# A row-mean kernel: the last tile's chunks summed by VectorE alone with a chained two-source instruction

## The chip, the cores and the metric

The kernel runs on 1 core of one Trainium2 chip. The metric is the device time of one execution in microseconds (us). The jobs ran on different chips (the record numbers them 13, 9, 2 and 4), so the verdicts rest on times of the same job.

Because the change works on the last 8 us or so, I also use a **tail**, read from the timeline of a trace. It runs from the start of the VectorE reduction of 128x4096 (I call that moment T0) to the issue of the last output store. That reduction starts when the last whole-tile load has landed, and the change does not touch it. The tail therefore leaves out all differences in the load stream before T0. A chunk's **landing** is the moment at which the trace records the load's last semaphore update; the `--critical` view ends a DMA piece there.

## The reference

```python
def setup_inputs():
    return {"x": np.random.randn(64, 256, 8192).astype(np.float32)}

def reference(x):
    return np.mean(x, axis=2)
```

These are 16384 rows of 8192 numbers, 537 MB read, and one mean per row written.

## The kernel before

Rows go on the 128 partitions. 63 loads bring two rows per partition each (128x16384). VectorE sums 62 of them with one reduction each and shares the 63rd with ScalarE. Then follow two tiles of 128 rows. The first comes in one load and is split between VectorE and ScalarE. The last comes in four chunks of falling size, so that little work is left when the last byte lands. The parts that the change touches:

```python
CH = [9 * L // 16, L // 4, L // 8, L // 16]      # 4608, 2048, 1024, 512 columns
...
s0 = CH[0] // 2 - L // 64                        # VectorE's share of chunk 0: 2176 columns
s1 = CH[1] // 2                                  # and of chunk 1: 1024
...
# VectorE
eng.wait_ge(one_sem, 16)
eng.tensor_reduce(res1[:, 0:1], buf1[:, : L // 2], X, ADD).then_inc(dve_sem, 1)   # 128x4096: T0
eng.wait_ge(ch_sems[0], 16)
eng.tensor_reduce(part[:, 0:1], buf2[:, :s0], X, ADD).then_inc(dve_sem, 1)
eng.wait_ge(ch_sems[1], 16)
eng.tensor_reduce(part[:, 1:2], buf2[:, offs[1] : offs[1] + s1], X, ADD).then_inc(dve_sem, 1)
eng.wait_ge(ch_sems[3], 16)
eng.tensor_reduce(part[:, 2:3], buf2[:, offs[3] : offs[3] + CH[3]], X, ADD).then_inc(dve_sem, 1)
eng.wait_ge(dve_sem, NP + 4)
eng.wait_ge(act_sem, 5)
eng.wait_ge(prep_sem, 1)
eng.tensor_reduce(fin[:, 0:1], part[:, 0:6], X, ADD).then_inc(fin_sem, 1)      # merge
eng.wait_ge(fin_sem, 1)
eng.transpose(fint[:], fin[:]).then_inc(fin_sem, 1)                            # column to rows
eng.wait_ge(fin_sem, 2)
eng.tensor_scalar(fint[:], fint[:], inv, None, mult).then_inc(fin_sem, 1)      # scale by 1/L
...
# ScalarE: the rest of chunks 0 and 1, and all of chunk 2, by accumulating copies
eng.wait_ge(ch_sems[0], 16)
acc(part[:, 3:4], buf2[:, s0 : CH[0]])
eng.wait_ge(ch_sems[1], 16)
acc(part[:, 4:5], buf2[:, offs[1] + s1 : offs[1] + CH[1]])
eng.wait_ge(ch_sems[2], 16)
acc(part[:, 5:6], buf2[:, offs[2] : offs[2] + CH[2]])
...
# SyncE: the last store
eng.wait_ge(fin_sem, 3)
eng.dma_start(out_q[4 * T2 : 4 * T2 + 4, :], fint[0:P:32, :])
```

Of the kernel before, what the change touches and what calls it, by code (L numbers as in the profile page):

```python
# [6 lines left out]
def bass_global_avg_pool_1d_kernel(  # L7
# [4 lines left out]
    P = 128  # L12
    B, C, L = x.shape
    rows = B * C
    inv = 1.0 / float(L)
    f32 = mybir.dt.float32
    ADD = mybir.AluOpType.add
    X = mybir.AxisListType.X
# [6 lines left out]
    assert rows % (R * P) == 0  # L25
    NP = rows // (R * P) - 1
    NBUF = 3
    CH = [9 * L // 16, L // 4, L // 8, L // 16]
    assert sum(CH) == L
    NCH = len(CH)  # L30

# [10 lines left out]
    with ExitStack() as ctx:  # L42
        E = ctx.enter_context
        bufs = [E(nc.sbuf_tensor(f"buf{i}", [P, R * L], f32)) for i in range(NBUF)]
        res = E(nc.sbuf_tensor("res", [P, NP, R], f32))
        res1 = E(nc.sbuf_tensor("res1", [P, 2], f32))
        part = E(nc.sbuf_tensor("part", [P, 8], f32))
        fin = E(nc.sbuf_tensor("fin", [P, 32], f32))
        fint = E(nc.sbuf_tensor("fint", [P, 32], f32))
        ident = E(nc.sbuf_tensor("ident", [P, P], f32))  # L50
        outsb = E(nc.sbuf_tensor("outsb", [NP, P, R], f32))
        out1sb = E(nc.sbuf_tensor("out1sb", [1, P], f32))
        ps = [E(nc.psum_tensor(f"ps{r}", [NP, P], f32)) for r in range(R)]
        psone = E(nc.psum_tensor("psone", [1, P], f32))

        in_sems = [E(nc.semaphore(f"in_sem{i}")) for i in range(NBUF)]
        one_sem = E(nc.semaphore("one_sem"))
        ch_sems = [E(nc.semaphore(f"ch_sem{i}")) for i in range(NCH)]
        dve_sem = E(nc.semaphore("dve_sem"))
        act_sem = E(nc.semaphore("act_sem"))  # L60
        prep_sem = E(nc.semaphore("prep_sem"))
        pe_sem = E(nc.semaphore("pe_sem"))
        cp_sem = E(nc.semaphore("cp_sem"))
        fin_sem = E(nc.semaphore("fin_sem"))
        out_sems = [E(nc.semaphore(f"out_sem{i}")) for i in range(3)]

        b1 = NP % NBUF
        b2 = (NP + 1) % NBUF
        buf1 = bufs[b1]
        buf2 = bufs[b2]  # L70
        offs = [sum(CH[:i]) for i in range(NCH)]
        s0 = CH[0] // 2 - L // 64
        s1 = CH[1] // 2

        def gpsimd_program(eng):
            eng.memset(fin[:], 0.0).then_inc(prep_sem, 1)  # L76
            eng.memset(ident[:], 0.0).then_inc(prep_sem, 1)  # L77
            eng.wait_ge(prep_sem, 2)
            eng.affine_select(  # L79
                out=ident[:],  # L80
                in_=ident[:],
                compare_op=mybir.AluOpType.not_equal,
                fill=1.0,
                base=0,
                pattern=[[-1, P]],
                channel_multiplier=1,
            ).then_inc(prep_sem, 1)

        first = len(nc.main_func.blocks[0].instructions)

        def sync_program(eng):
            for t in range(NP):
                if t >= NBUF:
                    eng.wait_ge(dve_sem, t - NBUF + 1)
                eng.dma_start(bufs[t % NBUF][:], x_pair[t]).then_inc(in_sems[t % NBUF], 16)  # L95
            eng.wait_ge(dve_sem, NP - NBUF + 1)
            eng.dma_start(buf1[:, :L], x_one[T1]).then_inc(one_sem, 16)
            eng.wait_ge(dve_sem, NP - NBUF + 2)
            for c in range(NCH):
                sl = slice(offs[c], offs[c] + CH[c])  # L100
                eng.dma_start(buf2[:, sl], x_one[T2][:, sl]).then_inc(ch_sems[c], 16)  # L101

            eng.wait_ge(cp_sem, 2)
            eng.dma_start(out_pair[0:NP, :], outsb[:].rearrange("t p r -> t (p r)")).then_inc(
                out_sems[0], 16
            )
            eng.wait_ge(cp_sem, 3)
            eng.dma_start(out_one[T1 : T1 + 1, :], out1sb[:]).then_inc(out_sems[1], 16)
            eng.wait_ge(fin_sem, 3)
            eng.dma_start(out_q[4 * T2 : 4 * T2 + 4, :], fint[0:P:32, :]).then_inc(  # L110
                out_sems[2], 16
            )
            for s in out_sems:
                eng.wait_ge(s, 16)

        def vector_program(eng):
            for t in range(NP - 1):
                eng.wait_ge(in_sems[t % NBUF], 16 * (t // NBUF + 1))
                eng.tensor_reduce(  # L119
                    res[:, t, :],  # L120
                    bufs[t % NBUF][:].rearrange("p (r l) -> p r l", r=R),
                    X,
                    ADD,
                ).then_inc(dve_sem, 1)
            t = NP - 1
            eng.wait_ge(in_sems[t % NBUF], 16 * (t // NBUF + 1))
            eng.tensor_reduce(res[:, t, 0:1], bufs[t % NBUF][:, :L], X, ADD).then_inc(dve_sem, 1)  # L127
            eng.wait_ge(one_sem, 16)
            eng.tensor_reduce(res1[:, 0:1], buf1[:, : L // 2], X, ADD).then_inc(dve_sem, 1)  # L129
            eng.wait_ge(ch_sems[0], 16)  # L130
            eng.tensor_reduce(part[:, 0:1], buf2[:, :s0], X, ADD).then_inc(dve_sem, 1)  # L131
            eng.wait_ge(ch_sems[1], 16)
            eng.tensor_reduce(  # L133
                part[:, 1:2], buf2[:, offs[1] : offs[1] + s1], X, ADD
            ).then_inc(dve_sem, 1)
            eng.wait_ge(ch_sems[3], 16)
            eng.tensor_reduce(  # L137
                part[:, 2:3], buf2[:, offs[3] : offs[3] + CH[3]], X, ADD
            ).then_inc(dve_sem, 1)
            eng.wait_ge(dve_sem, NP + 4)  # L140
            eng.wait_ge(act_sem, 5)
            eng.wait_ge(prep_sem, 1)
            eng.tensor_reduce(fin[:, 0:1], part[:, 0:6], X, ADD).then_inc(fin_sem, 1)  # L143
            eng.wait_ge(fin_sem, 1)
            eng.transpose(fint[:], fin[:]).then_inc(fin_sem, 1)  # L145
            eng.wait_ge(fin_sem, 2)
            eng.tensor_scalar(  # L147
                fint[:], fint[:], inv, None, mybir.AluOpType.mult
            ).then_inc(fin_sem, 1)

        def scalar_program(eng):
            def acc(dst, src):
                eng.activation(src, src, Copy, accum_out=dst).then_inc(act_sem, 1)  # L153

            t = NP - 1
            eng.wait_ge(in_sems[t % NBUF], 16 * (t // NBUF + 1))
            acc(res[:, t, 1:2], bufs[t % NBUF][:, L:])
            eng.wait_ge(one_sem, 16)
            acc(res1[:, 1:2], buf1[:, L // 2 : L])

            for r in range(R):
                eng.wait_ge(pe_sem, r + 1)
                eng.activation(outsb[:, :, r], ps[r][:], Copy, scale=inv).then_inc(cp_sem, 1)  # L163
            eng.wait_ge(pe_sem, 3)
            eng.activation(out1sb[:], psone[:], Copy, scale=inv).then_inc(cp_sem, 1)  # L165
            eng.wait_ge(ch_sems[0], 16)
            acc(part[:, 3:4], buf2[:, s0 : CH[0]])
            eng.wait_ge(ch_sems[1], 16)
            acc(part[:, 4:5], buf2[:, offs[1] + s1 : offs[1] + CH[1]])
            eng.wait_ge(ch_sems[2], 16)  # L170
            acc(part[:, 5:6], buf2[:, offs[2] : offs[2] + CH[2]])

        def tensor_program(eng):
            eng.wait_ge(prep_sem, 3)
            eng.wait_ge(dve_sem, NP)
            eng.wait_ge(act_sem, 1)
            for r in range(R):
                eng.transpose(ps[r][:], res[:, :, r], ident[:]).then_inc(pe_sem, 1)  # L178
            eng.wait_ge(dve_sem, NP + 1)
            eng.wait_ge(act_sem, 2)  # L180
            eng.matmul(psone[:], res1[:, 0:1], ident[:], start=True, stop=False)  # L181
            eng.matmul(psone[:], res1[:, 1:2], ident[:], start=False, stop=True).then_inc(pe_sem, 1)  # L182

        sync_program(nc.sync)
        gpsimd_program(nc.gpsimd)
        vector_program(nc.vector)
        scalar_program(nc.scalar)
        tensor_program(nc.tensor)



        stream = nc.main_func.blocks[0].instructions
        loads = stream[first : first + NBUF]
        del stream[first : first + NBUF]
        at = next(
            i
            for i, ins in enumerate(stream)
            if ins.engine == mybir.EngineType.SP and type(ins).__name__ == "InstDrain"
        )
        stream[at:at] = loads  # L200
# [28 lines left out]
```

## Time and profile before

| | before |
|---|---|
| time, median of 3 | 1247.26 us (1247.18 to 1247.38) |
| span of the profiled run | 1245.3 us |
| VectorE busy | 1085.6 us, 87% |
| VectorE idle before the 62 large reductions, for loads | 152.9 us |
| T0 to issue of the last store (tail) | 1243.62 - 1232.37 = 11.25 us |

Lines of the profile page of the kernel before: the span, each engine's busy time, DMA's busy tenths in 40 slices of the span, and the costliest group of instructions (line, engine, operation, shapes, count | busy us, mean ns | idle before and what ended it).

```profile
span 1245.3 us, 194 instructions
...
PE 1.7 (0%) x6; PEld 0.6 (0%) x6; DVE 1085.6 (87%) x70; ACT 17.2 (1%) x14; POOL 0.8 (0%) x7
...
DMA  9999999999999999999999999999999999999998
...
L119 DVE TENSOR_REDUCE res<-buf 128x2 f32<-128x16384 f32 x62 | 1067.6, 17220 | 152.9 <-DMA buf<-in_x_dram 152.9
...
```

DMA is at 9 tenths in all but the last slice, and VectorE's idle time ends with loads. The kernel is bound by its loads. With the loads left as they are, only what follows the last landing can be shortened. The chain of waits from 1200 us on (start, duration, what) shows that part:

```profile
...
1221.88 20.35 DMA buf<-in_x_dram
...
1242.26 0.70 DVE part L137
...
1242.98 0.17 DVE fin L143
...
1243.17 0.22 DVE fint L145
...
1243.42 0.18 DVE fint L147
```

After the last load (seen at 1242.23) come the reduction of 128x512, the merge, the transpose and the scale, each on the chain. The timeline of the same stretch (start, duration, engine, line, operation, shapes, and in brackets the idle time before it and its releaser):

```profile
...
1232.37 4.42 DVE L129 TENSOR_REDUCE res<-buf 128x1 f32<-128x4096 f32 x1 [1.02 <-DMA buf<-in_x_dram]
...
1241.63 1.06 ACT L153 ACTIVATE buf<-buf 128x1024 f32<-128x1024 f32 x1
1242.26 0.69 DVE L137 TENSOR_REDUCE part<-buf 128x1 f32<-128x512 f32 x1 [0.68 <-DMA buf<-in_x_dram]
...
1243.62 0.61 SPq L110 DMA_DIRECT2D out_dram<-fint  x1
```

L129 is T0. ScalarE's last piece starts at 1241.63 and is done with its accumulator read at 1242.78, before VectorE's last reduction ends at 1242.95, so ScalarE is not on the chain.

### The profile page before, as it was taken

The page shows a single profiled execution, that of the slowest core. Times are in us where ns is not written, and L with a number is a line of the kernel's source. Part 1 is how long each engine was busy: PE and PEld are TensorE (multiplying, and loading weights), DVE is VectorE, ACT ScalarE, POOL GpSimd, SP SyncE. Part 2 cuts the span into 40 slices and gives each one's busy share as a digit, 9 for nine tenths or more (in the row PEclk, how much of TensorE's full clock was granted, in tenths as well). Part 3 has the DMA queues.
Part 4 walks back from the last instruction along what each step waited for, and adds up shares of the span by engine and source line. Part 5 has one row for each costly group of instructions (what it writes and reads, how often), then busy time and mean ns, then how long its engine had stood idle before and what let it go on. Part 6 is the DMA issues. An engine that isn't in the chain of part 4 may idle for free.

```text
span 1245.3 us, 194 instructions
## 1 busy us (share of the span) xinstructions
PE 1.7 (0%) x6; PEld 0.6 (0%) x6; DVE 1085.6 (87%) x70; ACT 17.2 (1%) x14; POOL 0.8 (0%) x7
## 2 busy tenths in 40 slices
PE   0000000000000000000000000000000000000000
PEld 0000000000000000000000000000000000000000
DVE  2898988988889889898898988989889898898897
ACT  0000000000000000000000000000000000000005
POOL 0000000000000000000000000000000000000000
DMA  9999999999999999999999999999999999999998
GB/s 434 421 425 438 438 438 438 436 421 423 438 438 438 438 438 436 410 434 438 438 438 438 438 432 413 436 438 438 436 438 438 421 423 438 438 438 436 438 438 341
DMA packets 9876, 536.95 MB, mean 431 GB/s; under 512 B 1107, under 2 KB 1171, under 8 KB 1427
## 3 DMA queue, kind: packets, MB, share of 16 engines
q1 hardware_dynamic: 9874, 536.94, 99.7%
q14 instruction: 2, 0.01, 0.0%
HBM read 536.87 MB, written 0.07 MB: 431 GB/s over the span
## 4 chain that ended last, share of the span: by engine, by line
DMA 70%; DVE 29%; SPq 0%; issue 0%
DMA buf<-in_x_dram 70%; DVE res L119 29%; SPq L101 0%; DVE part L137 0%; SPq L95 0%; DVE fint L145 0%; DVE fint L147 0%; DVE fin L143 0%
## 5 line engine op out<-in xcount | busy, mean ns | idle before, releaser
L119 DVE TENSOR_REDUCE res<-buf 128x2 f32<-128x16384 f32 x62 | 1067.6, 17220 | 152.9 <-DMA buf<-in_x_dram 152.9
L153 ACT ACTIVATE buf<-buf 128x1024 f32<-128x1024 f32 (+3 forms) x5 | 15.0, 2994 | 1222.3 <-DMA buf<-in_x_dram 1222.2
L127 DVE TENSOR_REDUCE res<-buf 128x1 f32<-128x8192 f32 x1 | 8.7, 8686 | 2.1 <-DMA buf<-in_x_dram 2.1
L129 DVE TENSOR_REDUCE res<-buf 128x1 f32<-128x4096 f32 x1 | 4.4, 4420 | 1.0 <-DMA buf<-in_x_dram 1.0
L131 DVE TENSOR_REDUCE part<-buf 128x1 f32<-128x2176 f32 x1 | 2.4, 2419 | 1.1 <-DMA buf<-in_x_dram 1.1
L178 PE MATMUL ps<-ident,res 128*63 128x128 f32 x2 | 0.7, 430 | 1231.5 <-DVE res L127 1231.5
L153 ACT ACT_TABLE_LOAD x1 | 1.3, 1283 | 1.8 <-PEq L214 1.8
L133 DVE TENSOR_REDUCE part<-buf 128x1 f32<-128x1024 f32 x1 | 1.2, 1219 | 0.1
L137 DVE TENSOR_REDUCE part<-buf 128x1 f32<-128x512 f32 x1 | 0.7, 687 | 0.7 <-DMA buf<-in_x_dram 0.7
L153 ACT ACTIVATION_READ_ACCUMULATOR buf<-buf 128x1 f32 x5 | 0.9, 186 | 0.0
L178 PEld LDWEIGHTS ps<-ident,res 128*63 128x63 f32 x2 | 0.3, 205 | 1231.4 <-issue 1231.4
L182 PE MATMUL psone<-ident,res 128*1 128x128 f32 x2 | 0.6, 421 | 0.0
L181 PE MATMUL psone<-ident,res 128*1 128x128 f32 x2 | 0.6, 397 | 4.7 <-DVE res L129 4.7
L163 ACT ACTIVATE outsb<-ps 63x128 f32<-63x128 f32 x2 | 0.4, 264 | 0.0
L79 POOL TENSOR_SCALAR_AFFINE_SELECT ident<-ident 128x128 f32<-128x128 f32 x1 | 0.3, 292 | 0.2 <-POOL ident L77 0.2
L165 ACT ACTIVATE out1sb<-psone 1x128 f32<-1x128 f32 x1 | 0.3, 267 | 1.5 <-PE psone L182 1.5
L182 PEld LDWEIGHTS psone<-ident,res 128*1 128x1 f32 x2 | 0.3, 128 | 0.2
L145 DVE STREAM_TRANSPOSE fint<-fin 128x32 f32<-128x32 f32 x1 | 0.2, 212 | 0.0
L147 DVE TENSOR_SCALAR fint<-fint 128x32 f32<-128x32 f32 x1 | 0.2, 181 | 0.0
L77 POOL MEMSET ident<- 128x128 f32 x1 | 0.2, 204 | 0.0
L143 DVE TENSOR_REDUCE fin<-part 128x1 f32<-128x6 f32 x1 | 0.2, 158 | 0.0
L76 POOL MEMSET fin<- 128x32 f32 x1 | 0.1, 125 | 1.3 <-POOLq L214 1.3
(5 smaller groups left out, 0.5 us busy)
## 6 DMA issues: line engine op xcount, KB each, us to landing
buf<-in_x_dram SPq DMA_DIRECT2D x1, 4096.0 KB, 31.1
buf<-in_x_dram SPq DMA_DIRECT2D x1, 2304.0 KB, 17.3
buf<-in_x_dram SPq DMA_DIRECT2D x1, 1024.0 KB, 19.4
buf<-in_x_dram SPq DMA_DIRECT2D x63, 40.8
buf<-in_x_dram SPq DMA_DIRECT2D x1, 512.0 KB, 20.2
buf<-in_x_dram SPq DMA_DIRECT2D x1, 256.0 KB, 20.3
out_dram<-outsb SPq DMA_DIRECT2D x1, 63.0 KB
out_dram<-out1sb SPq DMA_DIRECT2D x1, 0.5 KB
```

Source lines behind the costliest of these rows:

```text
L79: eng.affine_select(out=ident[:], in_=ident[:], compare_op=mybir.AluOpType.not_equal, fill=1.0, base=0, pattern=[[-1, P]], channel_multipl ...
L119: eng.tensor_reduce(res[:, t, :], bufs[t % NBUF][:].rearrange("p (r l) -> p r l", r=R), X, ADD,).then_inc(dve_sem, 1)
L127: eng.tensor_reduce(res[:, t, 0:1], bufs[t % NBUF][:, :L], X, ADD).then_inc(dve_sem, 1)
L129: eng.tensor_reduce(res1[:, 0:1], buf1[:, : L // 2], X, ADD).then_inc(dve_sem, 1)
L131: eng.tensor_reduce(part[:, 0:1], buf2[:, :s0], X, ADD).then_inc(dve_sem, 1)
L133: eng.tensor_reduce(part[:, 1:2], buf2[:, offs[1] : offs[1] + s1], X, ADD).then_inc(dve_sem, 1)
L137: eng.tensor_reduce(part[:, 2:3], buf2[:, offs[3] : offs[3] + CH[3]], X, ADD).then_inc(dve_sem, 1)
L153: eng.activation(src, src, Copy, accum_out=dst).then_inc(act_sem, 1)
L163: eng.activation(outsb[:, :, r], ps[r][:], Copy, scale=inv).then_inc(cp_sem, 1)
L178: eng.transpose(ps[r][:], res[:, :, r], ident[:]).then_inc(pe_sem, 1)
L181: eng.matmul(psone[:], res1[:, 0:1], ident[:], start=True, stop=False)
L182: eng.matmul(psone[:], res1[:, 1:2], ident[:], start=False, stop=True).then_inc(pe_sem, 1)
```

## The change

The intent: VectorE reads two halves of a chunk at once, adds them, scales by 1/L and accumulates, in one instruction. Each instruction starts from the sum that the one before it left (`scalar`, the accumulator's first value). So the merge and the scale at the end go, and ScalarE's part goes. The chunks are resized so that one chunk's work about covers the next chunk's transfer.

```diff
--- before.py
+++ after.py
@@ -25,7 +25,8 @@
     assert rows % (R * P) == 0
     NP = rows // (R * P) - 1
     NBUF = 3
-    CH = [9 * L // 16, L // 4, L // 8, L // 16]
+
+    CH = [33 * L // 64, 65 * L // 256, 19 * L // 128, 21 * L // 256]
     assert sum(CH) == L
     NCH = len(CH)
 
@@ -44,7 +45,7 @@
         bufs = [E(nc.sbuf_tensor(f"buf{i}", [P, R * L], f32)) for i in range(NBUF)]
         res = E(nc.sbuf_tensor("res", [P, NP, R], f32))
         res1 = E(nc.sbuf_tensor("res1", [P, 2], f32))
-        part = E(nc.sbuf_tensor("part", [P, 8], f32))
+        part = E(nc.sbuf_tensor("part", [P, NCH], f32))
         fin = E(nc.sbuf_tensor("fin", [P, 32], f32))
         fint = E(nc.sbuf_tensor("fint", [P, 32], f32))
         ident = E(nc.sbuf_tensor("ident", [P, P], f32))
@@ -69,8 +70,6 @@
         buf1 = bufs[b1]
         buf2 = bufs[b2]
         offs = [sum(CH[:i]) for i in range(NCH)]
-        s0 = CH[0] // 2 - L // 64
-        s1 = CH[1] // 2
 
         def gpsimd_program(eng):
             eng.memset(fin[:], 0.0).then_inc(prep_sem, 1)
@@ -106,7 +105,7 @@
             )
             eng.wait_ge(cp_sem, 3)
             eng.dma_start(out_one[T1 : T1 + 1, :], out1sb[:]).then_inc(out_sems[1], 16)
-            eng.wait_ge(fin_sem, 3)
+            eng.wait_ge(fin_sem, 1)
             eng.dma_start(out_q[4 * T2 : 4 * T2 + 4, :], fint[0:P:32, :]).then_inc(
                 out_sems[2], 16
             )
@@ -127,26 +126,27 @@
             eng.tensor_reduce(res[:, t, 0:1], bufs[t % NBUF][:, :L], X, ADD).then_inc(dve_sem, 1)
             eng.wait_ge(one_sem, 16)
             eng.tensor_reduce(res1[:, 0:1], buf1[:, : L // 2], X, ADD).then_inc(dve_sem, 1)
-            eng.wait_ge(ch_sems[0], 16)
-            eng.tensor_reduce(part[:, 0:1], buf2[:, :s0], X, ADD).then_inc(dve_sem, 1)
-            eng.wait_ge(ch_sems[1], 16)
-            eng.tensor_reduce(
-                part[:, 1:2], buf2[:, offs[1] : offs[1] + s1], X, ADD
-            ).then_inc(dve_sem, 1)
-            eng.wait_ge(ch_sems[3], 16)
-            eng.tensor_reduce(
-                part[:, 2:3], buf2[:, offs[3] : offs[3] + CH[3]], X, ADD
-            ).then_inc(dve_sem, 1)
-            eng.wait_ge(dve_sem, NP + 4)
-            eng.wait_ge(act_sem, 5)
-            eng.wait_ge(prep_sem, 1)
-            eng.tensor_reduce(fin[:, 0:1], part[:, 0:6], X, ADD).then_inc(fin_sem, 1)
-            eng.wait_ge(fin_sem, 1)
+
+
+            for c in range(NCH):
+                lo, mid, hi = offs[c], offs[c] + CH[c] // 2, offs[c] + CH[c]
+                last = c == NCH - 1
+                eng.wait_ge(ch_sems[c], 16)
+                eng.wait_ge(dve_sem, NP + 1 + c)
+                if last:
+                    eng.wait_ge(prep_sem, 1)
+                eng.tensor_tensor_reduce(
+                    out=buf2[:, lo:mid],
+                    in0=buf2[:, lo:mid],
+                    in1=buf2[:, mid:hi],
+                    scale=inv,
+                    scalar=part[:, c - 1 : c] if c else 0.0,
+                    op0=ADD,
+                    op1=ADD,
+                    accum_out=fin[:, 0:1] if last else part[:, c : c + 1],
+                ).then_inc(dve_sem, 1)
+            eng.wait_ge(dve_sem, NP + 1 + NCH)
             eng.transpose(fint[:], fin[:]).then_inc(fin_sem, 1)
-            eng.wait_ge(fin_sem, 2)
-            eng.tensor_scalar(
-                fint[:], fint[:], inv, None, mybir.AluOpType.mult
-            ).then_inc(fin_sem, 1)
 
         def scalar_program(eng):
             def acc(dst, src):
@@ -163,12 +163,6 @@
                 eng.activation(outsb[:, :, r], ps[r][:], Copy, scale=inv).then_inc(cp_sem, 1)
             eng.wait_ge(pe_sem, 3)
             eng.activation(out1sb[:], psone[:], Copy, scale=inv).then_inc(cp_sem, 1)
-            eng.wait_ge(ch_sems[0], 16)
-            acc(part[:, 3:4], buf2[:, s0 : CH[0]])
-            eng.wait_ge(ch_sems[1], 16)
-            acc(part[:, 4:5], buf2[:, offs[1] + s1 : offs[1] + CH[1]])
-            eng.wait_ge(ch_sems[2], 16)
-            acc(part[:, 5:6], buf2[:, offs[2] : offs[2] + CH[2]])
 
         def tensor_program(eng):
             eng.wait_ge(prep_sem, 3)
```

## The prediction

> **What bounds the kernel now.** The loads. The page's slices show DMA at 9 in all but the last slice, about 438 GB/s in undisturbed slices; VectorE is busy 87% but always ends up waiting for data (152.9 us idle before the 62 large reductions, all of it for loads). The change touches neither these loads nor these reductions, so about 1237 us of the span of 1245.3 us cannot move. What can move is what follows the landing of the last chunk. The chain of waits there, in order: last load seen by VectorE at 1242.23; reduction of 128x512, 0.70; merge 0.17; transpose 0.22; scale 0.18; gaps of 0.02 to 0.03; the output store is issued at 1243.62 and takes the remaining 1.7 us (issue 0.61 plus landing).
>
> **What the change removes.** After the last chunk: the merge and the scale with their gaps, 0.19 + 0.20 = about 0.4 us. ScalarE's three pieces (2.2, 1.06, 1.06 us) go too, but ScalarE ended at 1242.78, before VectorE's last reduction at 1242.95, so that is worth nothing now.
>
> **What it adds.** VectorE must take all 8192 columns alone, two per step. One-source reductions here fit 152 ns + 1.04 ns per column (512: 687 ns, 1024: 1219, 2176: 2419). If the two-source instruction does one pair per cycle, it costs about 152 + 1.04 per pair, plus, as an estimate, 0.1 us for reading the accumulator (ScalarE's such read is 186 ns in the trace): 2.45, 1.33, 0.88 and 0.60 us. [...]The trace of before has no such instruction, so it cannot decide. The chunk sizes only make sense at one pair per cycle (each chunk's work about covers the next chunk's transfer); I give that 85%.
>
> **Critical path.** At the tail's roughly 410 GB/s the first chunk lands about 0.45 us earlier than now (about 1237.4), the others at about 1240.0, 1241.5 and 1242.3. VectorE is free at 1236.8. One pair per cycle: ends at about 1239.9, 1241.3, 1242.4, then 1243.0; transpose to 1243.25; store issued at 1243.27 instead of 1243.62. The last instruction is about as long as the one it replaces, since it has 336 pairs instead of 512 columns but also an accumulator read; so the gain is nearly only the two small instructions: 0.35 us. At half rate VectorE falls behind the loads from the first chunk on (4.6 + 2.4 + 1.5 + 1.0 us) and the kernel is some 3.5 us slower, 1250.8 us.
>
> **Prediction.** 1246.9 us, 8 in 10 between 1246.2 and 1248.2 us. Faster by over 2%: 0.3%; within 2%: 99.4%; slower by over 2%: 0.3%. Even the bad case is only 0.3%.
>
> **What would show it.** Right: large reductions unchanged (17.22 us each); two-source instructions of about 2.35, 1.25, 0.8 and 0.5 us; VectorE waiting for a load before chunk 2 and within 0.2 us of one before the last; the chain ends load, last two-source instruction, transpose, store; from the last landing to the store's issue about 1.0 us instead of 1.39. Wrong: a first two-source instruction of 4.4 us or more, or VectorE going from chunk to chunk without waiting.
>
> **What would make it wrong.** Half rate; a larger fixed cost of this instruction or its accumulator read (four in a row, the last two on the path); [...]a drift of the whole load stream between runs, as 0.1% of it is more than the change's effect.

Its sum: 1247.26 us of the kernel before, less the 0.35 us by which the last store is issued earlier (1243.62 - 1243.27), comes to 1246.9 us. Two passages are cut. "One pair per cycle" means there one pair in the 1.04 ns that a one-source reduction took per column; the 85% was the author's estimate. "Half rate" was an assumption for the bad case, not shown by any trace at that time: its durations are the author's estimate, from twice 1.04 ns per pair.

## The result, and the profile after

First comparison: 1246.30 us median of 4 (1246.09 to 1247.16) against 1247.22 us of 4 (1246.54 to 1247.38), ratio 0.9995, 95% interval 0.9978 to 1.0012. Second, of five rounds (run `after_again`): 1246.80 us (1246.35 to 1247.03) against 1246.88 us of 9, ratio 0.9999, interval 0.9986 to 1.0011. The medians differ by 0.92 us the first time and by 0.08 us the second, so the measured times do not resolve the effect. The predicted 1246.9 us with its range of 1246.2 to 1248.2 held both times. The kernel before, at 1247.22 and 1246.88 us, lies in that range too, so the range alone would have held without any gain.

The page of the kernel after:

```profile
span 1244.5 us, 194 instructions
...
PE 1.7 (0%) x6; PEld 0.6 (0%) x6; DVE 1086.1 (87%) x73; ACT 12.7 (1%) x8; POOL 0.8 (0%) x7
...
L118 DVE TENSOR_REDUCE res<-buf 128x2 f32<-128x16384 f32 x62 | 1067.6, 17220 | 152.5 <-DMA buf<-in_x_dram 152.5
...
```

The 62 large reductions are the same to the nanosecond in the mean (17220). ScalarE's busy time fell from 17.2 to 12.7 us and nothing came of it directly. The spans differ by 0.8 us, but 0.36 us of that arose before T0 (1232.37 against 1232.01), where the two programs do the same. The chain of waits and the timeline of the kernel after:

```profile
...
1241.88 0.13 issue
1242.02 0.57 DVE buf L138
...
1242.63 0.21 DVE fint L149
```

```profile
...
1232.01 4.42 DVE L128 TENSOR_REDUCE res<-buf 128x1 f32<-128x4096 f32 x1 [1.05 <-DMA buf<-in_x_dram]
...
1237.06 2.36 DVE L138 CUSTOM_DVE_ANT_0 buf<-buf 128x2112 f32<-128x2112 f32 x1 [0.62 <-DMA buf<-in_x_dram]
...
...
1239.57 1.30 DVE L138 CUSTOM_DVE_ANT_0 buf<-buf,part 128x1040 f32<-128x1040 f32 x1
...
1241.03 0.85 DVE L138 CUSTOM_DVE_ANT_0 buf<-buf,part 128x608 f32<-128x608 f32 x1
1241.80 0.08 DVE L138 DVE_READ_ACCUMULATOR2_ANT part<- 128x1 f32 x1
1242.02 0.57 DVE L138 CUSTOM_DVE_ANT_0 buf<-buf,part 128x336 f32<-128x336 f32 x1
1242.51 0.08 DVE L138 DVE_READ_ACCUMULATOR2_ANT fin<- 128x1 f32 x1
1242.63 0.21 DVE L149 STREAM_TRANSPOSE fint<-fin 128x32 f32<-128x32 f32 x1
1242.87 0.61 SPq L109 DMA_DIRECT2D out_dram<-fint  x1
```

Three readings:

- The tail is 1242.87 - 1232.01 = 10.86 us, against 11.25 before: 0.39 us less. It repeated as 10.87 in the second profile, taken in another job, while T0 itself varied between 1231.97 and 1232.54 us over all the profiles here. So the tail resolves hundredths of a us where the time does not.
- The chain of waits no longer begins with a load, as it did before. It stops at "issue", 0.13 us in which the profile shows nothing that VectorE waited for.
- Each two-source instruction comes with a short record of 82 to 84 ns, DVE_READ_ACCUMULATOR2_ANT, whose output is the column for its sum, in `part` or `fin` (below: the accumulator read). It lies at the instruction's end: the last one runs from 1242.51 to 1242.59, the instruction from 1242.02 to 1242.59. There is a pause of 0.13 to 0.15 us between each accumulator read's end and the next two-source instruction (for the last: 1241.80 + 0.08 to 1242.02), whereas the transpose follows the last accumulator read after 0.04 us.

### The profile page after: what moved, and what is told of

It reads as the page before. It is cut to its first block, busy times and chain, and to the rows that moved or that the text cites. A ratio compares the mean times of both kernels' runs of the same rounds, so it can differ in the third digit from the quotient of the medians. Undisturbed runs are those within 1.5% of the kernel's fastest.

```text
span 1244.5 us, 194 instructions
## 1 busy us (share of the span) xinstructions
PE 1.7 (0%) x6; PEld 0.6 (0%) x6; DVE 1086.1 (87%) x73; ACT 12.7 (1%) x8; POOL 0.8 (0%) x7
## 5 line engine op out<-in xcount | busy, mean ns | idle before, releaser
L118 DVE TENSOR_REDUCE res<-buf 128x2 f32<-128x16384 f32 x62 | 1067.6, 17220 | 152.5 <-DMA buf<-in_x_dram 152.5
L153 ACT ACTIVATE buf<-buf 128x8192 f32<-128x8192 f32 (+1 forms) x2 | 10.6, 5322 | 1221.9 <-DMA buf<-in_x_dram 1221.9
L138 DVE CUSTOM_DVE_ANT_0 buf<-buf,part 128x1040 f32<-128x1040 f32 (+2 forms) x3 | 2.7, 907 | 0.4
L138 DVE CUSTOM_DVE_ANT_0 buf<-buf 128x2112 f32<-128x2112 f32 x1 | 2.4, 2359 | 0.6 <-DMA buf<-in_x_dram 0.6
```

The source lines that it names most:

```text
L118: eng.tensor_reduce(res[:, t, :], bufs[t % NBUF][:].rearrange("p (r l) -> p r l", r=R), X, ADD,).then_inc(dve_sem, 1)
L138: eng.tensor_tensor_reduce(out=buf2[:, lo:mid], in0=buf2[:, lo:mid], in1=buf2[:, mid:hi], scale=inv, scalar=part[:, c - 1 : c] if c else 0 ...
L153: eng.activation(src, src, Copy, accum_out=dst).then_inc(act_sem, 1)
```

## The experiments

**Theory A**, the prediction's: loads set the starts of the two-source instructions, and the gain is the merge and the scale. **Theory B**: VectorE's own chain (its pauses, and the first value read from memory, which the recorded texts call the pointer) sets the end, and the equal sum is partly luck of other terms. All numbers below count from T0 of their own trace unless said. Each run is correct against the reference unless said.

### Where do the chunks land? (e1_probe)

```diff
             eng.activation(out1sb[:], psone[:], Copy, scale=inv).then_inc(cp_sem, 1)
+            for c in range(NCH):
+                hi = offs[c] + CH[c]
+                eng.wait_ge(ch_sems[c], 16)
+                eng.activation(probe[:, c : c + 1], buf2[:, hi - 1 : hi], Copy)
```

> The changed kernel with four tiny ScalarE copies, each released by one chunk's landing, so that ScalarE's starts show when the chunks land; ScalarE is idle there. All times count from the start of the 128x4096 reduction (T0). Before: last load seen at 9.86, last store issued at 11.25. After: two-source starts at 5.05, 7.56, 9.02 and 10.01, last store issued at 10.86. Theory A (as predicted: each two-source instruction waits for its chunk): chunks 2, 3 and 4 are seen by ScalarE within 0.05 us of the two-source starts. Theory B (VectorE's own chain, with 0.13 us gaps and an extra start cost for the pointer scalar, sets the starts): they are seen at least 0.1 us earlier, the second chunk by more; the last one at about 9.86.

Timeline of this run:

```profile
...
1232.48 4.42 DVE L129 TENSOR_REDUCE res<-buf 128x1 f32<-128x4096 f32 x1 [1.04 <-DMA buf<-in_x_dram]
...
1240.03 0.20 ACT L170 ACTIVATE probe<-buf 128x1 f32<-128x1 f32 x1 [1.67 <-DMA buf<-in_x_dram]
1240.04 1.30 DVE L139 CUSTOM_DVE_ANT_0 buf<-buf,part 128x1040 f32<-128x1040 f32 x1
...
1241.50 0.20 ACT L170 ACTIVATE probe<-buf 128x1 f32<-128x1 f32 x1 [1.27 <-DMA buf<-in_x_dram]
1241.51 0.85 DVE L139 CUSTOM_DVE_ANT_0 buf<-buf,part 128x608 f32<-128x608 f32 x1 [0.16 <-DMA buf<-in_x_dram]
1242.28 0.08 DVE L139 DVE_READ_ACCUMULATOR2_ANT part<- 128x1 f32 x1
1242.30 0.20 ACT L170 ACTIVATE probe<-buf 128x1 f32<-128x1 f32 x1 [0.60 <-DMA buf<-in_x_dram]
1242.50 0.57 DVE L139 CUSTOM_DVE_ANT_0 buf<-buf,part 128x336 f32<-128x336 f32 x1
...
1243.35 0.62 SPq L110 DMA_DIRECT2D out_dram<-fint  x1
```

The second and third chunks are seen by ScalarE within 0.01 us of the VectorE starts, as theory A says. But these starts also come 0.15 and 0.17 us after the accumulator read before them, which is about as long as the pause: landing and chain tie there, and e1 alone does not say which one sets the start. (e3 below, without the chain, starts these two instructions at 7.54 and 9.01, against 7.56 and 9.02 in the changed kernel, so the chain costs at most 0.02 us there.) The last chunk is seen at 1242.30 (9.82), but its instruction starts at 1242.50, after the third one's accumulator read ended at 1242.36 and a pause of 0.13 to 0.14 us. So at the end, where it counts, theory B holds, by 0.20 us. Tail 10.87: the probes disturbed nothing. The resized chunks are so well balanced that the loads and VectorE's chain tie until the last chunk.

### No chain, with and without the wait for the own predecessor (e2_imm_selfwait, e3_imm_nowait)

```diff
 # e2
-                    scalar=part[:, c - 1 : c] if c else 0.0,
+                    scalar=0.0,
-                    accum_out=fin[:, 0:1] if last else part[:, c : c + 1],
+                    accum_out=part[:, c : c + 1],
 ...
+            eng.wait_ge(prep_sem, 1)
+            eng.tensor_reduce(fin[:, 0:1], part[:, 0:NCH], X, ADD).then_inc(fin_sem, 1)
+            eng.wait_ge(fin_sem, 1)
 # e3, in addition
-                eng.wait_ge(dve_sem, NP + 1 + c)
```

> No chain by the accumulator's first value: all four start from an immediate 0 into four columns, merged by a 128x4 reduction at the end; the wait of each two-source instruction for the one before it is kept. If the pointer scalar costs the extra fixed time, the last three take 60 ns less each (about 1.24, 0.79 and 0.51 us); if the pointer also causes the gaps of 0.13 us, they shrink to about 0.02; if the wait for the own predecessor causes them, they stay. Theory A (loads set the starts): last store issued about 0.1 us later than after's 10.86 from T0, as the merge is added. Theory B: 0.1 us or more of the merge is won back.

> As the run with immediates, and without the waits for the own predecessor (each writes its own column, so none is needed). If that wait causes the gaps of 0.13 us they fall to about 0.02 where VectorE is behind the loads. Theory B: VectorE's chain is then short enough that it waits for the last chunk, the trace shows an idle time before the last two-source instruction put down to a load, and the merge eats the gain: last store issued at 10.8 to 10.9 from T0, as after. Theory A: no earlier start of any two-source instruction than after, last store issued at about 11.0.

Measured in e2: the last three instructions take 1243, 792 and 509 ns against 1302, 851 and 569 with the first value read from memory, so that read costs 59 to 60 ns each. The pause before the last one is still there (0.14 us), so the pointer does not cause it. Tail 10.93: the two theories' figures lie too close together here, so on that point the run decides nothing.

The chain of waits of e2 shows the pause in its parts (the accumulator read before it ends at 1242.02 to 1242.03, the last two-source instruction starts at 1242.17):

```profile
...
1242.04 0.03 issue
1242.06 0.02 DVEq L135
1242.09 0.08 issue
...
```

DVEq is the profile's name for VectorE's sequencer, and L135 is the line of the wait for the predecessor. What this record is, is taken up below under "Where the pause comes from".

The last two-source instruction of e3:

```profile
...
1242.23 0.51 DVE L135 CUSTOM_DVE_ANT_0 buf<-buf 128x336 f32<-128x336 f32 x1
...
```

Measured in e3: the last two-source instruction starts 9.82 after T0, which is when the probe saw the last chunk land, and without a pause. Tail 10.80. So without the chain the kernel is bound by the load at its end, and it pays for the merge and is still 0.06 us ahead of the change. I had expected the trace to show idle time before the last instruction, put down to a load. It shows none: VectorE became free just as the chunk landed. The trace's landing records confirm the load as the limit: all four two-source instructions of e3 start 0.02 us after the landing of their chunk.

### The old chunk sizes (e4_old_chunks, e7_old_imm_nowait)

```diff
 # e4: the changed kernel; e7: e3
-    CH = [33 * L // 64, 65 * L // 256, 19 * L // 128, 21 * L // 256]
+    CH = [9 * L // 16, L // 4, L // 8, L // 16]
```

> The changed kernel with the chunk sizes of before (4608, 2048, 1024, 512 columns). Theory A (loads set the starts): the last chunk lands at the same time and its instruction is shorter by 80 pairs or 0.08 us, so the last store is issued up to 0.1 us earlier than after. Theory B (VectorE's chain sets the end): the chain has the same number of pairs but starts 0.45 us later, as the first chunk is larger, so the last store is issued about 0.4 us later than after, at about 11.3 from T0, which gives the whole gain back.

> Chunk sizes of before, immediates, no waits for the own predecessor, merge at the end: VectorE is behind the loads from the second chunk on, so its bare gaps show. With the waits and the old sizes the three gaps were 0.14, 0.15 and 0.13 us. If the wait for the own predecessor causes them: all three fall to about 0.02, and the last store is issued about 11.33 - 3 x 0.18 + 0.19 = 10.98 from T0. If the instruction itself starts late whatever it waits for: they stay, and the store is issued at about 11.33.

Timeline of e4, where the chain and its waits stand:

```profile
...
1237.86 2.56 DVE L138 CUSTOM_DVE_ANT_0 buf<-buf 128x2304 f32<-128x2304 f32 x1 [1.10 <-DMA buf<-in_x_dram]
...
1242.69 0.08 DVE L138 DVE_READ_ACCUMULATOR2_ANT part<- 128x1 f32 x1
1242.90 0.48 DVE L138 CUSTOM_DVE_ANT_0 buf<-buf,part 128x256 f32<-128x256 f32 x1
...
1243.67 0.62 SPq L109 DMA_DIRECT2D out_dram<-fint  x1
```

And of e7, with immediates and without the waits:

```profile
...
1242.36 0.08 DVE L135 DVE_READ_ACCUMULATOR2_ANT part<- 128x1 f32 x1
1242.37 0.43 DVE L135 CUSTOM_DVE_ANT_0 buf<-buf 128x256 f32<-128x256 f32 x1
...
1243.27 0.62 SPq L109 DMA_DIRECT2D out_dram<-fint  x1
```

e4's tail is 1243.67 - 1232.34 = 11.33: theory B's 11.3, and 0.08 us **longer than before the change**. With the old sizes the first chunk starts at 5.52 instead of 5.05, and VectorE is behind from there to the end. Resizing the chunks is thus worth 11.33 - 10.86 = 0.47 us, more than the whole gain.

e7 shows what the chain costs. In e4 the last instruction starts 0.13 us after the end of the accumulator read before it (1242.77 to 1242.90). In e7 it starts at 1242.37, while that read still runs (to 1242.44): 0.07 us before its end. So at this place the wait for the own predecessor costs about 0.2 us, and the pointer 0.06 us more (485 against 426 ns for 256 pairs). By the landing records all four starts of e7, too, come 0.02 us after their chunk (the last: landed 9.87, started 9.89). Without the chain the loads set every start, and an even earlier start was not to be had. e7's tail is 10.79, less than the 10.98 that I expected, since I had not foreseen the overlap with the accumulator read. With no chain, the old and the new sizes give the same (10.79 and 10.80). The resizing only makes up for what the chain costs.

### The predicted gain alone (e5_before_cut)

```diff
 # on the kernel before; wrong result on purpose
-                part[:, 2:3], buf2[:, offs[3] : offs[3] + CH[3]], X, ADD
+                fin[:, 0:1], buf2[:, offs[3] : offs[3] + CH[3]], X, ADD
             ).then_inc(dve_sem, 1)
             eng.wait_ge(dve_sem, NP + 4)
-            eng.wait_ge(act_sem, 5)
-            eng.wait_ge(prep_sem, 1)
-            eng.tensor_reduce(fin[:, 0:1], part[:, 0:6], X, ADD).then_inc(fin_sem, 1)
-            eng.wait_ge(fin_sem, 1)
             eng.transpose(fint[:], fin[:]).then_inc(fin_sem, 1)
-            ... (the scale)
```

(The wait for the memset of `fin` moved ahead of that reduction.)

> The kernel before without the merge and the scale; ScalarE's and VectorE's split, instructions and chunks stay. Wrong result on purpose: the last 128 sums lack ScalarE's parts and the scale. This is the part of the change that the prediction counted, alone. Theory A (the gain is the two removed instructions): last store issued at 11.25 - 0.39 = 10.86 from T0 (start of the 128x4096 reduction), the same as the changed kernel. If something else costs or pays, it lies more than 0.05 away from 10.86.

```profile
...
1232.13 4.42 DVE L129 TENSOR_REDUCE res<-buf 128x1 f32<-128x4096 f32 x1 [1.03 <-DMA buf<-in_x_dram]
...
1242.97 0.62 SPq L110 DMA_DIRECT2D out_dram<-fint  x1
```

The tail is 1242.97 - 1232.13 = 10.84 us. The result is wrong. Removing merge and scale is worth 0.41 us, and it equals the full change's gain within 0.02 us.

### One source instead of two (e6_one_source)

```diff
-                eng.tensor_tensor_reduce(out=..., in0=buf2[:, lo:mid], in1=buf2[:, mid:hi], ...)
+                eng.tensor_reduce(part[:, c : c + 1], buf2[:, lo:hi], X, ADD).then_inc(dve_sem, 1)
 ... no waits for the predecessor; merge and scale again at the end
```

> VectorE alone on the new chunks, but with the one-source reduction, then merge and scale: what the change would be without the paired reading. From 152 ns + 1.04 ns per column: 4.55, 2.32, 1.42, 0.85 us, starting at 5.05 from T0 without waiting for loads, so 14.2, then merge, transpose and scale: last store issued at about 14.9 from T0, 4.0 us later than the changed kernel, about 1250.5 us in all. Anything below 13 would mean that the two-source instruction is not what lets one engine keep up.

```profile
...
1237.01 8.87 DVE L134 TENSOR_REDUCE part<-buf 128x1 f32<-128x4224 f32 x4 [0.62 <-DMA buf<-in_x_dram]
...
1246.56 0.62 SPq L109 DMA_DIRECT2D out_dram<-fint  x1
```

The tail is 14.59 us, 3.7 us longer than after, and the one time 1249.86 us against 1247.11 us of the kernel before in the same job. (The four durations behind the expected 14.9 add up to 9.14 us; the four took 8.87 us from the first start to the last end.) So reading in pairs is what lets VectorE do the chunks alone.

### An attempt to beat both (v1_shared, v3_four, v3_four_direct, and the repeats)

The chain is cut another way. The last chunk gets a tile of its own with six columns in front, and all partial sums of VectorE and ScalarE are written into those columns. The last two-source instruction then sums them along with the data. The excerpt is condensed; the waits for the predecessor go too, except before the last instruction.

```diff
+    last = E(nc.sbuf_tensor("last", [P, NX + CH[-1]], f32))   # NX = 6
+    CH = [3968, 2176, 1216, 512, 320]; SH = [0, 0, 400, 160, 0]   # SH: ScalarE's columns
-                    scale=inv, scalar=part[:, c - 1 : c] if c else 0.0, accum_out=...
+                    scale=1.0, scalar=0.0, accum_out=last[:, c : c + 1],      # chunks but the last
+            eng.tensor_tensor_reduce(out=last[:, :h], in0=last[:, :h], in1=last[:, h:],
+                scale=inv, scalar=0.0, op0=ADD, op1=ADD, accum_out=fin[:, 0:1])
 # v3_four: CH = [4864, 2048, 768, 512]; SH = [480, 600, 200, 0]
 # v3_four_direct, in addition: no transpose, the store reads fin[:, 0:1]
```

> An attempt to beat both: five chunks (3968, 2176, 1216, 512, 320 columns), no chain; ScalarE takes 400 and 160 columns of the third and fourth; all partial sums are written next to the last chunk in its own tile, so that the last two-source instruction (163 pairs, scale 1/L) sums them along with the data. The last chunk should land at about 9.82 from T0 as ever. If the self wait costs its 0.14 us again, the last instruction starts at about 9.95 and ends about 10.28, transpose, store issued at about 10.55: 0.3 us before the changed kernel, too little to show in one time (about 1246.4 us). If landing or ScalarE is later than worked out, the idle time before the last two-source instruction says which.

> The five-chunk attempt issued its last store 10.67 from T0, not 10.55: its fourth chunk landed 0.3 us before the last, and the last instruction waited for ScalarE's piece of it. Here four chunks (4864, 2048, 768, 512), ScalarE takes 480, 600 and 200 columns of the first three, the last instruction has 259 pairs. If the landing of the last chunk (9.82) sets its start: it ends at about 10.26, store issued at about 10.55. If the wait for the own predecessor or for ScalarE still comes last, it starts at 9.95 or later and the store is issued at 10.65 or later, no better than five chunks.

> The same without the transpose: the last store takes 128 single values from 128 partitions. It is issued 0.24 us earlier (about 10.3 from T0). If the store of 128 runs of 4 bytes lasts no longer than that of 4 runs of 128 bytes (1.63 us from issue to the span's end), the span's end comes 0.24 us earlier too; if it takes longer by more than that, the transpose is worth keeping.

v1_shared has a tail of 10.67 us, 0.19 us less than the changed kernel, but not the 10.55 of the estimate. I had put this down to ScalarE's piece of the fourth chunk (the timeline names ScalarE) and planned v3_four for it; its tail is 10.70. The chain of waits names the load instead, in both. Of v3_four:

```profile
...
1221.53 20.35 DMA last<-in_x_dram
1241.89 0.03 DVEq L154
1241.92 0.08 issue
...
```

The last chunk landed at 1241.89 (9.87, against 9.86 before the change), but its instruction starts at 1242.00, 0.11 us later, although its predecessor's accumulator read had ended at 1241.74. In v1_shared the landing is at 1242.04 (9.94) and the start at 1242.16. So both forms pay a pause after the landing (0.11 and 0.12 us) that e3 and e7 (0.02 us) do not have, and they come out about equal.

v3_four_direct issued its store at 10.46 from T0, 0.24 us earlier than v3_four (expected about 10.3), and its span is 1250.0 against 1244.4 us. The store in its timeline:

```profile
...
1242.44 0.36 SPq L113 DMA_DIRECT2D out_dram<-fin  x1
```

From 1242.44 to the span's end at 1250.0 is 7.6 us for a store of 128 single values, against 1244.4 - 1242.72 = 1.7 us with the transpose and runs of 128 bytes. The transpose of 0.21 us earns 5.6 us (one run of each).

Then the changed kernel and v1 again, side by side on one chip, five rounds each:

> The changed kernel again, five rounds beside the kernel before. From the tail (10.86 against 11.25 from T0 to the last store's issue) the difference should be 0.4 us, ratio 0.9997. One execution of one kernel differs from another by up to 1 us, so the interval may well contain 1; the trace's tail should repeat within 0.05 us (10.81 to 10.91).

> The five-chunk version with ScalarE's share and the sums within the last tile, five rounds. Its tail was 10.67, so 0.58 us faster than before and 0.19 us faster than the changed kernel; ratio to before 0.9995. The trace's tail should repeat within 0.05 us; by the clock the two new kernels may not be told apart.

| tail (us) | profile 1 | profile 2 | five rounds, median (range) | ratio to before, 95% |
|---|---|---|---|---|
| before | 11.25 | | 1246.88 (1246.52 to 1247.33, 9 runs) | |
| after | 10.86 | 10.87 | 1246.80 (1246.35 to 1247.03) | 0.9999 (0.9986 to 1.0011) |
| v1 | 10.67 | 10.67 | 1246.16 (1246.07 to 1246.40) | 0.9995 (0.9981 to 1.0008) |

Timeline of v1_again:

```profile
...
1232.45 4.42 DVE L132 TENSOR_REDUCE res<-buf 128x1 f32<-128x4096 f32 x1 [1.03 <-DMA buf<-in_x_dram]
...
1242.51 0.33 DVE L155 CUSTOM_DVE_ANT_0 last<-last 128x163 f32<-128x163 f32 x1 [0.17 <-ACT buf L170]
...
1243.12 0.62 SPq L113 DMA_DIRECT2D out_dram<-fint  x1
```

The tails repeat within 0.01 us: 1243.12 - 1232.45 = 10.67 for v1. All its five times lie below all nine of before, but the interval contains 1, so the tail is the evidence that it is ahead, not the time.

### Where the pause comes from

The traces hold records that the timeline leaves out; `--critical` and `--source` show them as DVEq. They are EVENT_SEMAPHORE instructions. In the traces of before and after, a VectorE instruction with several waits in the program has such records in front of it for all waits but the first (before: one of 552 ns at L142, for the merge's second and third wait; after: three of 21 ns at L135 and one of 821 ns at L137). Below, the instruction is said to carry the first wait, and the others are called separate. The chains of e2 and v3_four show the same records (L135 and L154, 0.02 and 0.03 us). In the changed kernel the program waits for the load first, so the wait for the predecessor is the separate one. In after, e2 and e4 the separate wait is over 0.05 to 0.06 us after the accumulator read's end, and the two-source instruction starts 0.08 to 0.09 us after that: that is the pause (0.13 to 0.15 us). In v3_four it is the load's wait that is separate and is over last (in v1_shared the landing at 1242.04 and the end of ScalarE's accumulator read at 1242.07 come close together before the start at 1242.16), and the same 0.08 to 0.09 us follow. Where the wait that ends last is the one that the instruction carries, the start follows after 0.02 us (a landing, e3 and e7) or 0.03 to 0.04 us (an accumulator read: the transpose, and the merge of e2, which also has a separate wait, but one that was over long before). So the pause goes with the separate wait and not with the predecessor as such. No run tests this directly: writing the wait for the predecessor first, and the load's second, was not tried.

## Why the prediction was right

**The bound: right.** Nothing before T0 changed, large reductions 17.22 us each as predicted, and the time moved by less than 0.1%.

**One pair per cycle (85%): right.** The trace shows 1.04 ns per pair, as for one column of a one-source reduction (512 columns 687 ns, 1024 columns 1219 ns). Durations predicted with the accumulator read: 2.45, 1.33, 0.88 and 0.60 us; measured 2.36, 1.30, 0.85 and 0.57, the read of 0.08 us lying within 0.01 us of the instruction's end (`after`). With an immediate first value, durations over four kernels fit 160 ns + 1.04 ns per pair (256 pairs 426 ns in e7, 336 pairs 509 ns and 1040 pairs 1243 ns in e2, 2112 pairs 2359 ns in after). The half rate that the prediction allowed for (4.4 us or more for the first instruction) does not show: 2112 pairs took 2359 ns.

**The landings: right within 0.11 us.** Predicted as 7.63, 9.13 and 9.93 after T0 (1240.0, 1241.5 and 1242.3 less 1232.37). The probe saw 7.55, 9.02 and 9.82. The odd chunk sizes did no visible harm: the last chunk was seen at 9.82, and before the change it landed at 9.86.

**"0.35 us" of gain: right, measured 0.39 in the tail.** The removed instructions alone give 0.41 (e5). From the last landing to the last store's issue: predicted 1.0 us, probe run 1243.35 - 1242.30 = 1.05 (from the probe's start, 0.02 us after the landing), before 1243.62 - 1242.23 = 1.39.

**"The last instruction is about as long as the one it replaces ... so the gain is nearly only the two small instructions": right as a sum, incomplete as an account.** The sequence of runs gives:

| step | tail, us | change |
|---|---|---|
| before | 11.25 | |
| merge and scale removed (e5, wrong result) | 10.84 | -0.41 |
| the whole change with the old chunk sizes (e4) | 11.33 | +0.49 |
| the chunk sizes of the change (after) | 10.86 | -0.47 |

The chain costs two things that the prediction did not have: 60 ns per instruction for the first value read from memory (e2), and about 0.2 us for waiting on the predecessor, measured at the last instruction (e4 against e7). At the second and third chunk all but 0.02 us of it is hidden behind the loads, thanks to the new sizes (7.56 and 9.02 in after, 7.54 and 9.01 in e3). Before the last instruction 0.20 us of it is exposed (e1). The step of +0.49 also hands ScalarE's columns to VectorE, but e7 does that too, without the chain, and has a tail of 10.79 with a merge still in it: the chain is what costs.

That the sum came out right is in part luck. The last instruction was predicted to start at 10.03 (1242.4) and started at 10.01. But the third chunk's instruction started 0.11 us earlier than predicted and was 0.03 us shorter, and this made up for a pause of 0.13 to 0.14 us that the prediction did not have. The durations, too, are right for a partly wrong reason: the 0.1 us estimated for the accumulator read is not needed, as the read overlaps the instruction's end, and the pointer's 0.06 us took most of its place.

**"The chain ends load, last two-source instruction, transpose, store": wrong in its first link.** The chain after ends in VectorE's own sequence; the last chunk had landed 0.20 us before. The prediction itself had VectorE free at 1242.4 against a landing at 1242.3, so the near tie was foreseen, but not that the pause would come on top. Of the prediction's own signs, "VectorE waiting for a load before chunk 2" did not appear either: the trace of after puts no idle time there down to a load, and each later start comes 0.13 to 0.15 us after an accumulator read. That is close to the sign it gave for being wrong, "going from chunk to chunk without waiting".

What stays open: why a start after a separate wait takes 0.06 us more than one after a carried wait (0.08 to 0.09 against 0.02 us), and whether the other order of the two waits would remove it.

## What to carry to other kernels

When a change trades one small serial cost for another at the end of a load-bound kernel, measure from a fixed event near the end (here the last whole-tile reduction) to the last store: it repeated within 0.01 us where times of whole runs spread over 1 us. Here each link of a chain of dependent instructions on one engine had its price (a pause of 0.13 to 0.15 us, and 0.06 us for the first value); separate accumulators and one merge were as good (tail 10.80 against 10.86 us), and partial sums written next to the last data and summed with it were better (10.67 us). Resize chunks together with the change of the work per chunk: with the chain it was worth more (0.47 us) than the instructions removed (0.41 us), without the chain nothing. And where an instruction has several waits, look in the chain of waits for the sequencer's separate ones (DVEq) before blaming the engine that the timeline names.
